# The value products of sparse attention, issued in eight rows of eight instead of sixteen rows of four

## The chip, the cores and the metric

One core of a Trainium2 chip (trn2) runs the whole layer. The metric is the device time of one execution in microseconds; the kernel before has a median of 1277.29 us over 3 runs (1276.85 to 1277.38).

## What the reference computes

One decoder layer (sequence 256, width 2048, all float32): a mixer, cross-attention to 256 memory tokens, and a gated MLP, each followed by a layer norm. The mixer projects the input and feeds three groups side by side: a diagonal state-space model (S5), stick-breaking attention, and NSA, attention with 16 query heads in 4 groups that share keys and values. NSA is the part that matters here. Its three branches (compressed keys, selected blocks, sliding window) are added with gates:

```python
p_s = masked_softmax(s_s, (dist_s >= 0)[:, :, None])
o_s = jnp.einsum('bgrqm,bgqmd->bqgrd', p_s.astype(vs.dtype), vs)
...
p_w = masked_softmax(s_w, mask_w)
o_w = jnp.einsum('bgrqk,bkgd->bqgrd', p_w.astype(vwb.dtype), vwb)
...
o = gb[..., 0:1] * o_c + gb[..., 1:2] * o_s + gb[..., 2:3] * o_w
```

With 256 tokens there are 4 blocks of 64, all of which are selected, and the window of 512 covers every earlier token, so the selected and the window branch are both plain causal attention, each with its own keys and values. The change is in their products of probabilities and values.

## The kernel before, in words

The program is written with a tile framework. Its planner puts the instructions of each engine in a fixed order when the kernel is built: it simulates the engines and issues, of what is ready, what has the best priority. Priorities go by lanes: `first`, then `split` (loads and the splitting of weights), `mixer` (attention and the like), and `proj` (the products of the projections), which so fills what the others leave free. `after(a, b)` adds that `a` is issued after `b`, without a semaphore; `in_row(row)` does it for a list, each after the one before. An engine runs its instructions in the order that was fixed.

The projections multiply float32 values split into a high and a low part: ScalarE casts a chunk of 1024 columns of weights to `hi` (line 304), VectorE takes the rest as `lo` (line 305), and three products are issued for each piece (`mm3`, lines 319 to 321, tokens moving; `mm3x`, lines 327 to 329, weights moving). Chunks come through four `raw` buffers and three each of `hi` and `lo`.

In the NSA stage 16 heads are worked through as 4 quads of 4. For each quad there are two branches `b` (0 is the selected one, which also gives the scores of the compressed keys, 1 the window), and in each branch two groups `gl` with two heads `r` each: 16 pairs of heads. For a head, TensorE forms scores (lines 1044 and 1045, into one of two `mx` banks), VectorE adds the bias and takes minima (1048, 1050), ScalarE the exponentials (1060, 1062), VectorE scales by gate and sum (1065 to 1069), TensorE transposes three blocks into one of two alternating banks `op` and `pb` (1074), and ScalarE copies them to a `pt` tile of 128 x 384 (1076). The products of line 1081 then multiply 64 columns of values `vv` (the weights) with `pt` (moving, 256 or 128 columns); head `r` = 0 writes partitions 0 to 63 of the bank `pa`, head 1 partitions 64 to 127, and group `gl` its own 256 columns. A float32 product is two load and two product records in the profile. At a quad's end the compressed branch is added (transposes 1092, copy 1096, products 1098), and `pa` is copied to `mix` (1101, 1102).

Projections fill the rest of this stage: the queries of NSA, `mix_out(0)` (first half of the output projection) and `memory_k` (keys of the memory, whose results `xk` are copied at line 1132). `mix_out(1)` comes behind the stage and reads NSA's `mix`. The stick-breaking stage before (`stick_breaking`) has four rows of its own at line 855, made with `in_row` and a dependency on ScalarE's last exponential.

Of the kernel before, what the change touches and what calls it, by code (L numbers as in the profile page):

```python
# [8 lines left out]
F32 = mybir.dt.float32  # L9
# [156 lines left out]
class Parts:  # L166
# [9 lines left out]
    def range(self, k, n):  # L176
        if k == 0 and self.first is not None:
            assert n == 1
            return self.first
        return self.tiles[k // self.n][:, k % self.n:k % self.n + n]  # L180
# [18 lines left out]
class Program:  # L199
# [322 lines left out]
    def mixer(self):  # L522
# [6 lines left out]
        with ExitStack() as nsa:  # L529
            self.nsq = pool(nsa, "nsq", 1)  # L530
            self.slabp = pool(nsa, "slabp", 1)
            with ExitStack() as s5:
                self.s5p = pool(s5, "s5p", 1, "right")
                self.s5w = pool(s5, "s5w", 2, "right")
                self.s5_tables()
                self.load_x()
                with ExitStack() as st:
                    self.sbp = pool(st, "sbp", 1)
                    self.sbw = pool(st, "sbw", 2)
                    self.stick_breaking()  # L540
                self.nsk = pool(nsa, "nsk", 1)
                self.nsa_compress()
                self.nsa_values()
                self.s5_out()
            self.resp = pool(self.ctx, "resp", 1, "right")
            self.R = self.resp.tile([128, 2, D], F32, name="R")
            self.mixq = pool(self.ctx, "mixq", 1, "right")
            self.mix += [self.mixq.tile([128, 4, 2, 256], F32R, name=f"mix{i}")
                         for i in range(2, 4)]
            with ExitStack() as st:  # L550
                self.nsp = pool(st, "nsp", 1, "right")
                self.nsw = pool(st, "nsw", 2, "right")
                self.nsa_queries()
                self.nsa()
# [452 lines left out]
    def nsa(self):  # L1007
        nc, a, V, S = self.nc, self.a, self.nc.vector, self.nc.scalar
        p, mm = self.nsp, nc.tensor.matmul
        vcb, vv, gate, ks, q = self.vcb, self.vv, self.gate, self.ks, self.nq  # L1010
        slab = self.slab
        self.after(S.activation(gate, gate, ACTF.Exp, scale=-1.0), self.table)
        V.tensor_scalar(gate, gate, 1.0, None, ALU.add)
        V.reciprocal(gate, gate)


        def qcol(h):
            return 4 * (h // 8) + 2 * (h // 4 % 2) + h % 2


        pc = p.tile([128, 2, NH, 32], F32, name="pc")
        nc.gpsimd.memset(pc, 0.0)
        tcs = [p.tile([128, 2, 4, NC_], F32, name=f"tcs{i}") for i in range(2)]
        for t in tcs:
            nc.gpsimd.memset(t[:, 0], BIG)
        halves = lambda t: t.rearrange("p (c k) -> p c k", c=2)
        for quad in range(4):
            o = self.pq.tile([128, 2, 256], F32, name="pa")
            start = [None, None]
            for b in range(2):  # L1030
                n = 128 if b else 128 + NK
                for gl in range(2):
                    h0, v = 4 * quad + 2 * gl, 4 * b + 2 * (quad // 2) + gl
                    sums = self.nsw.tile([128, 2, 2], F32, name="sums")
                    pes, pts = [], []
                    for r in range(2):
                        h = h0 + r
                        kh, kl = (k[:, h // 8, gl].rearrange("p c n -> p (c n)") for k in ks[b])
                        t = qcol(h)
                        z = self.mx.tile([128, 512], F32, name="mx")  # L1040

                        for qt, m in enumerate((256, n + 128)):
                            qs, zs = slice(128 * qt, 128 * qt + 128), z[:, qt * n:qt * n + m]
                            mm(zs, q[:, t, gl, qs], kh[:, 0:m], start=True, stop=False)  # L1044
                            mm(zs, q[:, t, gl, qs], kl[:, 0:m], start=False, stop=True)  # L1045
                        tt = self.nsw.tile([128, 384], F32, name="tt")
                        mn = self.nsw.tile([128, 2], F32, name="mn")
                        V.tensor_tensor_reduce(tt[:, 0:128], z[:, 0:128], slab[:, h, 128:256],
                                               1.0, 3e38, ALU.add, ALU.min, mn[:, 0:1])
                        V.tensor_tensor_reduce(halves(tt[:, 128:384]),  # L1050
                                               halves(z[:, n:3 * n])[:, :, 0:128],
                                               halves(slab[:, h, :]), 1.0, 3e38, ALU.add, ALU.min,
                                               mn[:, 1:2])
                        if b == 0:
                            for qt in range(2):
                                V.tensor_add(tcs[quad % 2][:, qt, 2 * gl + r, 0:NB[qt]],
                                             z[:, 128 + qt * n:128 + qt * n + NB[qt]],
                                             slab[:, h, 159 - 128 * qt:256:16])
                        pe = self.nsw.tile([128, 384], F32, name="pe", bufs=3)
                        S.activation(pe[:, 0:128], tt[:, 0:128], ACTF.Exp, scale=-1.0,  # L1060
                                     bias=mn[:, 0:1], accum_out=sums[:, r, 0:1])
                        S.activation(pe[:, 128:384], tt[:, 128:384], ACTF.Exp, scale=-1.0,
                                     bias=mn[:, 1:2], accum_out=sums[:, r, 1:2])
                        pes.append(pe)
                    V.reciprocal(sums, sums)
                    V.tensor_mul(sums, sums, gate[:, :, h0:h0 + 2, 1 + b].rearrange("p q r -> p r q"))
                    for r, pe in enumerate(pes):
                        V.tensor_scalar(pe[:, 0:128], pe[:, 0:128], sums[:, r, 0:1], None, ALU.mult)
                        V.tensor_scalar(pe[:, 128:384], pe[:, 128:384], sums[:, r, 1:2], None,
                                        ALU.mult)  # L1070
                        ps = self.turn()
                        for c in range(3):
                            cs = slice(c * 128, c * 128 + 128)
                            last = nc.tensor.transpose(ps[:, cs], pe[:, cs], self.ident)
                        pt = self.nsw.tile([128, 384], F32, name="pt", bufs=3)
                        S.copy(pt, ps[:, 0:384])
                        pts.append(pt)

                    for c, (k0, k1) in enumerate(((0, 256), (256, 384))):
                        for r, pt in enumerate(pts):  # L1080
                            ins = mm(o[64 * r:64 * r + 64, gl, 128 * c:256], vv[:, c, v, :],  # L1081
                                     pt[:, k0:k1], start=start[r] is None, stop=False,
                                     skip_group_check=True)
                            if c == 0:
                                self.after(ins, start[r] or last)
                                start[r] = start[r] or ins
                if b == 0:
                    self.softmax(tcs[quad % 2], gate[:, :, 4 * quad:4 * quad + 4, 0],
                                 pc[:, :, 4 * quad:4 * quad + 4, 0:NC_])
            ps = self.turn()  # L1090
            for qt in range(2):
                nc.tensor.transpose(ps[:, qt * 128:qt * 128 + 128],
                                    pc[:, qt, 4 * quad:4 * quad + 4, :].rearrange(
                                        "p r n -> p (r n)"), self.ident)
            pt = self.nsw.tile([128, 384], F32, name="pt", bufs=3)
            S.copy(pt[:, 0:256], ps[:, 0:256])
            for gl in range(2):
                mm(o[:, gl, :], vcb[:, quad // 2, 2 * gl:2 * gl + 2, :].rearrange("p r d -> p (r d)"),
                   pt[:, 0:256], start=False, stop=True, skip_group_check=True)
            m = self.mix[2 + quad // 2][:, quad % 2:4:2]  # L1100
            S.copy(m[:, :, 0, :], o)
            V.tensor_sub(m[:, :, 1, :], o, m[:, :, 0, :].bitcast(F32))
# [267 lines left out]
```

## Time and profile before

| what | us |
|---|---|
| median of 3 runs | 1277.29 |
| the profiled execution, its own time | 1276.8 |
| its span, first to last instruction | 1274.6 |
| mean granted TensorE clock over the span | 0.994 of full speed |
| NSA stage, from the span's start | 268 to 398 |

The times of the rows below are of the one profiled execution and count from its span's start. Its own time is 2.2 us longer than the span; the median of the runs is 0.5 us above it. PE is TensorE's matmul, PEld its weight loads, DVE is VectorE, ACT ScalarE, SP the queue that issues most loads. The ends of matmuls are modelled, so two that follow each other overlap in the rows in order of time; the chain of waits gives each only the time until the next.

### The profile page before, as it was taken

The page shows a single profiled execution, that of the slowest core. Times are in us where ns is not written, and L with a number is a line of the kernel's source. Part 1 is how long each engine was busy: PE and PEld are TensorE (multiplying, and loading weights), DVE is VectorE, ACT ScalarE, POOL GpSimd, SP SyncE. Part 2 cuts the span into 40 slices and gives each one's busy share as a digit, 9 for nine tenths or more (in the row PEclk, how much of TensorE's full clock was granted, in tenths as well). Part 3 has the DMA queues.
Part 4 walks back from the last instruction along what each step waited for, and adds up shares of the span by engine and source line. Part 5 has one row for each costly group of instructions (what it writes and reads, how often), then busy time and mean ns, then how long its engine had stood idle before and what let it go on. Part 6 is the DMA issues. An engine that isn't in the chain of part 4 may idle for free.

```text
span 1274.6 us, 23037 instructions
## 1 busy us (share of the span) xinstructions
PE 1242.8 (98%) x9222; PEld 1151.6 (90%) x9222; DVE 878.8 (69%) x1507; ACT 660.5 (52%) x1032; POOL 19.0 (1%) x34
## 2 busy tenths in 40 slices
PE   7999999999999999899999999999999999999996
PEld 7788889997788999799999999999999988888896
DVE  7799997876765766866666666666666654444557
ACT  6884446565663366365555555555555543334342
POOL 0200000100000000000000000000000000000000
PEclk9999999999999999999999999999999999999998
DMA  8654247664454655355666666666566766656573
GB/s 307 196 167 150 84 130 239 213 197 141 133 204 160 193 196 169 113 164 191 196 192 192 196 193 191 196 194 190 196 192 192 262 192 190 196 188 199 187 237 132
DMA packets 67350, 237.37 MB, mean 186 GB/s; under 512 B 7787, under 2 KB 8604, under 8 KB 66476
## 3 DMA queue, kind: packets, MB, share of 16 engines
q1 hardware_dynamic: 64720, 230.21, 55.9%
q0 software_dynamic: 1424, 4.33, 1.5%
q8 instruction: 72, 1.18, 0.4%
q10 hardware_dynamic: 1100, 1.38, 0.3%
q14 instruction: 34, 0.28, 0.1%
HBM read 231.82 MB, written 2.49 MB: 184 GB/s over the span
## 4 chain that ended last, share of the span: by engine, by line
PE 86%; DVE 6%; DMA 3%; ACT 3%; issue 2%; POOL 0%; DVEq 0%; ACTq 0%; POOLq 0%
PE pj L321 16%; PE pj L319 16%; PE pj L320 16%; PE pj L328 10%; PE pj L327 10%; PE pj L329 10%; PE pa L1081 2%; DVE s5m L191 1%; DVE lo L305 1%; DMA s5us<-Ec 1%; DVE s5z L191 1%; DMA raw<-in_win_u 1%; ACT hi L304 1%; PE mx L1044 1%; PE mx L1045 1%
## 5 line engine op out<-in xcount | busy, mean ns | idle before, releaser
L305 DVE TENSOR_TENSOR lo<-raw,hi 128x1024 fp32r<-128x1024 f32 (+2 forms) x403 | 488.1, 1211 | 330.4 <-ACT hi L304 329.2
L304 ACT CAST hi<-raw 128x1024 fp32r<-128x1024 f32 (+2 forms) x403 | 419.6, 1041 | 500.2 <-PE pj L320 268.1
L320 PE MATMUL pj<-mix,hi 128*128 128x256 f32 x1380 | 382.4, 277 | 0.0
L319 PE MATMUL pj<-mix,hi 128*128 128x256 f32 x1380 | 381.9, 277 | 0.0
L321 PE MATMUL pj<-mix,lo 128*128 128x256 f32 x1380 | 381.3, 277 | 0.0
L319 PEld LDWEIGHTS pj<-mix,hi 128*128 128x128 f32 x1380 | 259.5, 188 | 0.2
L320 PEld LDWEIGHTS pj<-mix,hi 128*128 128x128 f32 x1380 | 259.4, 188 | 0.1
L321 PEld LDWEIGHTS pj<-mix,lo 128*128 128x128 f32 x1380 | 259.4, 188 | 0.0
L319 PE MATMUL pj<-A,hi 128*128 128x256 f32 x496 | 139.6, 284 | 6.7 <-ACT hi L304 6.1
L321 PE MATMUL pj<-A,lo 128*128 128x256 f32 x496 | 137.6, 284 | 3.7 <-DVE lo L305 3.7
L320 PE MATMUL pj<-A,hi 128*128 128x256 f32 x496 | 138.6, 282 | 0.0
L319 PEld LDWEIGHTS pj<-A,hi 128*128 128x128 f32 x496 | 94.4, 191 | 9.4 <-ACT hi L304 6.6
L321 PEld LDWEIGHTS pj<-A,lo 128*128 128x128 f32 x496 | 92.9, 191 | 7.0 <-DVE lo L305 4.9
L328 PE MATMUL pj<-lo,A 128*128 128x512 f32 (+2 forms) x288 | 96.0, 334 | 1.0 <-DVE lo L305 1.0
L328 PE MATMUL pj<-lo,act 128*128 128x512 f32 (+1 forms) x280 | 96.3, 345 | 0.0
L329 PE MATMUL pj<-hi,act 128*128 128x512 f32 (+1 forms) x280 | 96.3, 345 | 0.0
L329 PE MATMUL pj<-hi,A 128*128 128x512 f32 (+2 forms) x288 | 95.8, 334 | 0.0
L320 PEld LDWEIGHTS pj<-A,hi 128*128 128x128 f32 x496 | 94.7, 192 | 0.8 <-issue 0.8
L327 PE MATMUL pj<-hi,A 128*128 128x512 f32 (+2 forms) x288 | 91.4, 334 | 0.6 <-ACT hi L304 0.6
L327 PE MATMUL pj<-hi,act 128*128 128x512 f32 (+1 forms) x280 | 89.3, 345 | 0.0
L328 PEld LDWEIGHTS pj<-lo,A 128*128 128x128 f32 x288 | 54.1, 188 | 7.8 <-DVE lo L305 1.5
L329 PEld LDWEIGHTS pj<-hi,A 128*128 128x128 f32 x288 | 54.2, 188 | 5.8 <-issue 0.8
(321 smaller groups left out, 1792.2 us busy)
## 6 DMA issues: line engine op xcount, KB each, us to landing
raw<-in_w_up SPq DMA_DIRECT2D x176, 512.0 KB, 4.4
raw<-in_w_down SPq DMA_DIRECT2D x92, 512.0 KB, 4.4
raw<-in_win_c SPq DMA_DIRECT2D x48, 512.0 KB, 4.1
raw<-in_w_out SPq DMA_DIRECT2D x32, 512.0 KB, 3.4
raw<-in_win_sv SPq DMA_DIRECT2D x8, 512.0 KB, 4.5
raw<-in_wk_m SPq DMA_DIRECT2D x8, 512.0 KB, 4.1
raw<-in_wv_m SPq DMA_DIRECT2D x8, 512.0 KB, 3.6
raw<-in_wq SPq DMA_DIRECT2D x8, 512.0 KB, 3.4
```

Source lines behind the costliest of these rows:

```text
L191: ins = getattr(self.engine, name)(*args, **kw)
L304: self.last_hi = nc.scalar.copy(hi[:, :n], raw[:, :n])
L305: self.last_lo = nc.vector.tensor_sub(lo[:, :n], raw[:, :n], hi[:, :n].bitcast(F32))
L319: mm(ps, hi, ah, start=start, stop=False)
L320: mm(ps, hi, al, start=False, stop=False)
L321: self.last_mm = mm(ps, lo, ah, start=False, stop=stop)
L327: mm(ps, ah, hi, start=start, stop=False)
L328: mm(ps, ah, lo, start=False, stop=False)
L329: self.last_mm = mm(ps, al, hi, start=False, stop=stop)
L1044: mm(zs, q[:, t, gl, qs], kh[:, 0:m], start=True, stop=False)
L1045: mm(zs, q[:, t, gl, qs], kl[:, 0:m], start=False, stop=True)
L1081: ins = mm(o[64 * r:64 * r + 64, gl, 128 * c:256], vv[:, c, v, :], pt[:, k0:k1], start=start[r] is None, stop=False, skip_group_check=True)
```

## The change

The products of a branch of a quad are issued after both of its groups have their four `pt` tiles, as one row of eight: for each of the two column pieces `c`, group 0 head 0, group 0 head 1, group 1 head 0, group 1 head 1. The row is put in order by `in_row`, and its first product waits, with a semaphore, for the last of the four copies (`copied`). Number, shapes and operands of the products stay as they were. The pool of `pt` tiles has five buffers in place of three.

```diff
@@ nsa() @@
             for b in range(2):
                 n = 128 if b else 128 + NK
+                pts = []
                 for gl in range(2):
-                    h0, v = 4 * quad + 2 * gl, 4 * b + 2 * (quad // 2) + gl
+                    h0 = 4 * quad + 2 * gl
                     sums = self.nsw.tile([128, 2, 2], F32, name="sums")
-                    pes, pts = [], []
+                    pes = []
...
-                        pt = self.nsw.tile([128, 384], F32, name="pt", bufs=3)
-                        S.copy(pt, ps[:, 0:384])
+                        pt = self.nsw.tile([128, 384], F32, name="pt", bufs=5)
+                        copied = S.copy(pt, ps[:, 0:384])
                         pts.append(pt)
 
-                    for c, (k0, k1) in enumerate(((0, 256), (256, 384))):
-                        for r, pt in enumerate(pts):
-                            ins = mm(o[64 * r:64 * r + 64, gl, 128 * c:256], vv[:, c, v, :],
+                row = []
+                for c, (k0, k1) in enumerate(((0, 256), (256, 384))):
+                    for gl in range(2):
+                        for r, pt in enumerate(pts[2 * gl:2 * gl + 2]):
+                            ins = mm(o[64 * r:64 * r + 64, gl, 128 * c:256],
+                                     vv[:, c, 4 * b + 2 * (quad // 2) + gl, :],
                                      pt[:, k0:k1], start=start[r] is None, stop=False,
                                      skip_group_check=True)
                             if c == 0:
                                 self.after(ins, start[r] or last)
                                 start[r] = start[r] or ins
+                            row.append(ins)
+                self.tc.add_manual_dep(row[0].ins, copied.ins.name, mybir.DependencyInfo(
+                    mybir.DependencyClass.Sync, mybir.DependencyReason.DATA), reason="in one row")
+                self.in_row(row)
...
-            pt = self.nsw.tile([128, 384], F32, name="pt", bufs=3)
+            pt = self.nsw.tile([128, 384], F32, name="pt", bufs=5)
             S.copy(pt[:, 0:256], ps[:, 0:256])
```

## Rows read from the trace of the kernel before

**Rows 1.** The page: the chain that ended last, shares of the span by line.
```profile
PE pj L321 16%; PE pj L319 16%; PE pj L320 16%; PE pj L328 10%; PE pj L327 10%; PE pj L329 10%; PE pa L1081 2%; DVE s5m L191 1%; DVE lo L305 1%; DMA s5us<-Ec 1%; DVE s5z L191 1%; DMA raw<-in_win_u 1%; ACT hi L304 1%; PE mx L1044 1%; PE mx L1045 1%
```
**Rows 2.** Windows: stretch, length, busy of PE, PEld, DVE, ACT, POOL, clock, DMA.
```profile
268.00:398.00 130.00, 129.05 (x870) 106.74 (x871) 94.28 (x343) 79.03 (x208) 0.00 (x0) 1.00 0.46 158
...
600.00:1200.00 600.00, 600.00 (x4499) 569.41 (x4498) 365.77 (x464) 292.85 (x380) 0.00 (x0) 1.00 0.62 197
```
**Rows 3.** Waits of SP's queue and DVE, 268 to 398: total, times, longest.
```profile
SPq L276 <- DVE lo L305: 71.2, 16, 7.6
...
DVE sums L1065 <- ACT pe L1062: 16.6, 9, 3.5
```
**Rows 4.** Groups by line, ACT, 268 to 398: busy, mean ns, idle before.
```profile
L304 ACT CAST hi<-raw 128x1024 fp32r<-128x1024 f32 x27 | 28.2, 1044 | 19.9 <-PE pj L329 14.1 <-PE pj L320 5.9
```
**Rows 5.** Line 1076, 268 to 398: what ended ACT's idle time, us, times.
```profile
  PE pb L1074: 11.4, 6
  PE op L1074: 8.8, 5
```
**Rows 6.** Groups by line, PE, 268 to 398.
```profile
L1081 PE MATMUL pa<-pt,vv 128*64 128x128 f32 (+1 forms) x128 | 22.2, 344 | 0.0
```
**Rows 7.** Chain of waits, 255 to 400, pieces of line 1081: start, us.
```profile
276.71 0.57 PE pa L1081 x2
278.52 0.79 PE pa L1081 x5
...
314.10 0.80 PE pa L1081 x8
```
**Rows 8.** PE in order of time, several stretches: start, us, instructions.
```profile
105.14 0.86 PE L855 MATMUL op<-sbe,sbv 128*64 128x256 f32 x6
...
106.37 0.43 PE L855 MATMUL op<-sbe,sbv 128*64 128x128 f32 x2
...
278.45 0.86 PE L1081 MATMUL pa<-pt,vv 128*64 128x256 f32 x6
...
288.82 0.38 PE L1074 MATMUL pb<-cst,pe 128*128 128x128 f32 x2
...
390.80 0.86 PE L1081 MATMUL pa<-pt,vv 128*64 128x256 f32 x6
391.60 0.39 PE L319 MATMUL pj<-A,hi 128*128 128x256 f32 x1
...
398.04 0.40 PE L327 MATMUL pj<-hi,mix 128*128 128x512 f32 x1
```
**Rows 9.** Chain of waits, projections before and behind line 1081.
```profile
276.59 0.11 PE pj L321
...
277.28 0.32 PE pj L319
...
279.31 0.31 PE pj L319
```
**Rows 10.** Chain of waits, a quad's products of line 1098.
```profile
336.78 0.86 PE pa L1098 x4
```
**Rows 11.** Line 1081, its weight loads: duration ns, least, median, greatest.
```profile
L1081 PEld LDWEIGHTS pa<-pt,vv x128: 132/136/137, 276.6 to 391.3; 128*64 128x64 f32 x128
```
**Rows 12.** PEld in order of time, from 313.95.
```profile
314.03 0.63 PEld L1081 LDWEIGHTS pa<-pt,vv 128*64 128x64 f32 x8 [0.37 <-DVE sums L1066]
```
**Rows 13.** Groups by line, PE, 100 to 200: the stick-breaking rows.
```profile
L855 PE MATMUL op<-sbe,sbv 128*64 128x256 f32 (+1 forms) x32 | 3.9, 340 | 0.5 <-ACT sbe L848 0.5
```
**Rows 14.** DVE in order of time, from 387; in brackets idle before.
```profile
390.91 1.09 DVE L1132 COPY xk<-pj 128x256 f32<-128x256 f32 x3 [2.05 <-PE pb L1092]
...
395.56 0.69 DVE L1102 TENSOR_TENSOR mix<-pa,mix 128x512 fp32r<-128x512 f32 x1 [2.43 <-ACT mix L1101]
```
**Rows 15.** ACT in order of time, two stretches.
```profile
290.11 0.47 ACT L1076 COPY pt<-pb 128x384 f32<-128x384 f32 x1
...
387.88 0.49 ACT L1076 COPY pt<-op 128x384 f32<-128x384 f32 x1
```

## The prediction

> **What bounds the kernel now.** I read the page first, then the stages, then the chain of waits inside the one stage that the diff touches. In the page's chain that ended last, TensorE's (PE's) lines 319 to 321 and 327 to 329, the projections, hold 3 x 16 + 3 x 10 = 78% of the span, and the touched products of line 1081 hold 2% [rows 1]. The windows view shows how even this is: in the NSA stage, 268 to 398 us, PE is busy 129.05 of 130 us at granted clock 1.00, while VectorE (DVE) has 94.28 and ScalarE (ACT) 79.03; from 600 to 1200 PE is busy 600 of 600 [rows 2]. In the NSA stage its own small work is spread over a stream of projection products, and these fill every hole. So here a microsecond that PE no longer needs is a microsecond off the end, if two things hold: the softmax chain on DVE and ACT keeps up with the quicker PE, and the loads do.
>
> The loads first. In this stage SP's queue waits 71.2 us for DVE's `lo` [rows 3], which frees a load buffer; DMA moves at 0.46 of its share [rows 2]. Loads wait for buffers, not PE for loads. ACT's cast of the next weights waits 19.9 us for PE to give a buffer back [rows 4]: the preparation of weights, too, stands on PE.
>
> The chain second. ACT waits 8.8 + 11.4 = 20.2 us, at 5 + 6 = 11 of the 32 copies to `pt`, for transposes that PE has not yet issued [rows 5]; DVE waits 16.6 us for exponentials that stand behind those copies [rows 3]. The chain is waiting for PE's order, not the other way round. PE itself shows 0.0 idle before line 1081 [rows 6].
>
> **What one group of products costs now.** A product is two records on PE, one for each weight load. The chain of waits shows a group of four products (eight records, two heads into the two halves of the array's columns) in two forms. In 13 of 16 groups the first head's first product goes off alone as "x2", other work follows, then the other three go ("x5" in the chain, six records in the order of time); in 3, the first groups of the second, third and fourth quad, the eight stand together; one of each kind is shown [rows 7, 8]. Each visit costs its own time and a slow return to the projections: the matmul behind takes 0.32 or 0.31 us in the chain where its like take 0.11 [rows 9].
> - alone: 0.57 + (0.32 - 0.11) = 0.78 us
> - the six: 0.79 + (0.31 - 0.11) = 0.99 us
> - the eight together, with the same return: 0.80 + 0.21 = 1.01 us
>
> The eight cost no more than the six because the halves run beside each other: the lone first product hides beside the other head's. Columns agree: four full-width records of 256 columns take 0.86 us [rows 10], 0.215 each. One half has two such records and two of half the width: 2 x 0.215 + 2 x 0.108 = 0.645 us, and 1.01 - 0.645 = 0.36 us is the price of going in and out. Alone: 0.43 + 0.35.
> Before, in all: 13 x (0.78 + 0.99) + 3 x 1.01 = 26.0 us.
>
> **The change, part by part.**
> *One row of eight.* Alternating heads keep both halves filled, so a row has two groups' columns and one way in and out: 1.01 + 0.645 = 1.65 us; eight rows make 13.2 us. PE saves 26.0 - 13.2 = 12.8 us: about 10 from 13 lone visits, 2.9 from eight other visits fewer. Number and shapes of products, loads and copies are unchanged.
>
> *A rule of the skill, weighed.* Eight weight loads of about 0.136 us each, 1.09 in sum [rows 11], end within 0.63 us of the first one's start [rows 12], and their products take 0.80 us [rows 7]: loads run beside loads and products. The Trainium skill ("TensorE: Matmul & The Clock Gate", Part 3, The mechanism) says that a weight load overlaps running matmuls only when its row group differs; all these products use all 128 rows, so by it the loads would add to the time. The trace disagrees, and the sum goes by the trace; by the rule the change would lose, as worked out under the rivals.
>
> *The wait at the row's head.* Its first product now waits for the last of four copies. Behind it in PE's queue stand projections, the next heads' scores and transposes; for these wait DVE's minima, ACT's copies, the casts. Below: 0, since PE idles 0.0 before line 1081 [rows 6]. Above: the stick-breaking stage has four rows made in this form (in order, waiting for ACT's last result), and there PE idled 0.5 us before them in total [rows 13]. All of that at one row and the same at each of eight gives 4.0 us; its mean, 0.125 us a row, gives 1.0. I take 1.0, the same form being the nearest row.
>
> *Products of the first pair move later,* by one pair, some 8 us. Only line 1098 and the copy to `mix` need them, at the quad's end, and these wait for the second pair anyhow: no cost. The last quad's mix is written at 395.56 to 396.25, the next consumer, `mix_out(1)`, starts at 398.04 [rows 8, 14], and its first chunks read other tiles.
>
> *Two more buffers.* Four copies are held until the row; the fifth takes the next head's copy or line 1096's. They run nothing. Were they missing, ACT would stand at the next copy: the 0.48 us of a copy and what waits for it.
>
> Sum: 1276.8 (the profiled execution, span 1274.6 and 2.2 around it) - 12.8 + 1.0 = 1265.0. The median of the runs stands 0.5 higher: **1265.5 us**. Bounds of the wait, and up to 1 us for the return cost of rows that end at transposes, make 1263.5 to 1268.5.
>
> **The rivals.**
> A. *The chain shows.* 11 of 32 copies waited for PE with 20.2 us in all, more than 12.8 [rows 5]; but if they stand for 11 of the 16 pairs, 5 pairs have no such cover. If these give their share back, 5/16 x 12.8 = 4.0 us: 1269.5. For: in `xk` too, DVE copies three finished blocks only at 390.91, released by the last quad's transposes, and the fourth block starts at 391.60 [rows 8, 14], so the stage's end has little play. Against: DVE would be busy 94.28 of some 117 us, 80%.
>
> B. *Halves not beside each other* in the longer row. 16 records in sequence: 8 x 0.215 + 8 x 0.108 + 0.36 = 2.94 us, 23.5 in all, 2.5 saved: 1274.8. Against: the eight at 0.80 [rows 7].
>
> C. *Loads show.* 16 loads x 0.136 = 2.2 us more a row, 17.4 in all, against 12.8: 4.6 lost, 1281.9. Against: the 0.63 us [rows 12]. This is what the skill's rule quoted above would make of it.
>
> D. *The row stands too early in PE's queue: slower.* Place: each row's head. After transposes that end at 289.20, the second copy ends at 290.58, as exponentials stand before it [rows 8, 15]: 1.4 us, and 2.4 with a 1.04 us cast [rows 4] in front. If rows are queued right behind the transposes, with nothing between, eight times this is 11.2 to 19.2 us: 1264.5 + 11.2 = 1275.7 to 1283.7. It decides from 12.8/8 = 1.6 us a row (gain gone). Against: the last group's copies end at 388.37 and its six records go at 390.80 [rows 8, 15]; projections stand between, and none of 16 groups kept PE idle [rows 6].
>
> E. *The rows do not come out whole.* One of the stick-breaking rows goes as six records and, after another line's, two [rows 8]. Eight extra visits of 0.36 leave 9.9 us of gain: 1268.4.
>
> **How the numbers follow.** Forecast 0.64, A 0.13, E 0.05, B 0.05, C 0.03, D 0.10. The forecast's own range is 1263.5 to 1268.5; with A and E up to 1271 it holds 0.82, and I open the low end to 1262.8, for PE work saved that the sum of visits misses. 0.2%, 2.6 us, is about what a measurement of this kernel can tell from no change. Faster: forecast, A, E and 0.02 of B, 0.84. Same: 0.03 of B and 0.06 of D, 0.09. Slower: C and 0.04 of D, 0.07.
>
> **What would show it.** Line 1081 as eight pieces of "x16" (or near) and about 1.44 us in the chain, the matmul behind at 0.3; no "x2" pieces; PE idle before line 1081 about 1 us; the start of `mix_out(1)` near 386 in place of 398.04; ACT's 20.2 us for transposes down to about half. Pieces of 2.7 us mean B or C; idle before line 1081 of over 4 us means D; idle before lines 1044, 1074 or 319 in the stage means A. The forecast is wrong above all if the queue's order in the stage changes so that projections run out before the last quad ends.

## The result, and the profile after

The kernel with the change takes 1265.42 us (median of 6 runs, 1264.3 to 1266.71), the kernel before beside it 1276.91 us (6 runs, 1275.76 to 1277.38). The ratio is 0.9911, 95% interval 0.9900 to 0.9922: 1276.91 x 0.0089 = 11.4 us, or 0.9%, faster. Forecast was 1265.5 us, 11.8 us below the 1277.29 us of before that were known then.

The profiled execution has a span of 1262.4 us. The windows view of it, with the columns of [rows 2]:

```profile
268.00:386.00 118.00, 116.57 (x870) 104.22 (x869) 92.77 (x331) 77.55 (x203) 0.00 (x0) 1.00 0.51 171
...
600.00:1190.00 590.00, 590.00 (x4403) 559.11 (x4402) 359.35 (x457) 287.04 (x371) 0.00 (x0) 1.00 0.60 197
```

The reader is to see that the stage which ran from 268 to 398 us ends at 386: 870 product records in 118 us, where before the same number, equal also shape by shape, took 130 [rows 2]. PE's busy time for them fell from 129.05 to 116.57 us, by 12.5 us, and its idle time rose from 0.95 to 1.43 us. Behind the stage PE is as full as before, so nothing of this is given back.

The products of line 1081 are line 1084 now. The chain of waits, 255 to 400 (start, us, what), against [rows 7]:

```profile
284.92 1.45 PE pa L1084 x16
286.37 0.48 PE op L1075 x3
286.85 0.33 PE pb L1075 x3
...
334.03 0.86 PE pa L1106 x4
334.89 0.33 PE pb L1075 x3
...
344.92 1.45 PE pa L1084 x16
346.38 0.32 PE pj L329
346.69 0.12 PE pj L327
...
378.18 1.52 PE pa L1084 x16
```

Eight pieces of sixteen records, seven of 1.45 us and the last of 1.52; predicted were 1.44. No pieces of two are left. The return is there too: the projection behind a row takes 0.32 us where the next takes 0.12, three transposes behind a row 0.48 where the next three take 0.33. PE in order of time around the first row and at the stage's end, against [rows 8]:

```profile
284.52 0.40 PE L327 MATMUL pj<-hi,mix 128*128 128x512 f32 x1
284.85 1.52 PE L1084 MATMUL pa<-pt,vv 128*64 128x256 f32 x16
286.31 0.55 PE L1075 MATMUL op<-cst,pe 128*128 128x128 f32 x3
...
376.49 0.61 PE L1075 MATMUL pb<-cst,pe 128*128 128x128 f32 x3 [1.25 <-DVE pe L1069]
376.95 0.61 PE L1075 MATMUL op<-cst,pe 128*128 128x128 f32 x3
377.72 0.44 PE L1100 MATMUL pb<-cst,pc 128*128 128x128 f32 x2 [0.17 <-ACT pt L1077]
378.18 1.52 PE L1084 MATMUL pa<-pt,vv 128*64 128x256 f32 x16
...
386.06 0.40 PE L327 MATMUL pj<-hi,mix 128*128 128x512 f32 x1
```

`mix_out(1)` starts at 386.06 in place of 398.04: 11.98 us of the difference between the spans (12.2) are there by then. The brackets show the only idle time of PE in the stage, 1.25 + 0.17 us. It stands not at a row's head but before the last transposes, at the stage's very end, where no projection is left to fill. Before, PE idled once in the stage too, at its start, and that wait is gone:

```profile
268.95 0.39 PE L1044 MATMUL mx<-kh,nq 128*128 128x256 f32 x1 [0.97 <-DVE tcs L1056]
```

ACT's waits in the stage (total, times, longest), against [rows 5]:

```profile
ACT pt L1077 <- PE pb L1075: 10.5, 6, 3.6
...
ACT pt L1077 <- PE op L1075: 4.2, 4, 1.5
```

ACT still waits for PE's transposes, 14.7 us in place of 20.2: the softmax chain has used 5.5 us of its play (time it spends waiting, and can lose without holding PE up). Over most of the stage it has not become the limit. At the end it has: the chain of waits leaves PE for 2.2 us, from 374.25 to 376.49:

```profile
374.25 0.35 ACT pt L1077
...
374.63 0.49 ACT pe L1061 x2
375.12 0.50 ACT pe L1063 x2
...
376.05 0.30 DVE pe L1069
```

### The profile page after: what moved, and what is told of

It reads as the page before. It is cut to its first block, busy times and chain, and to the rows that moved or that the text cites. A ratio compares the mean times of both kernels' runs of the same rounds, so it can differ in the third digit from the quotient of the medians.

```text
span 1262.4 us, 23018 instructions
## 1 busy us (share of the span) xinstructions
PE 1229.5 (97%) x9222; PEld 1149.0 (91%) x9222; DVE 878.8 (70%) x1507; ACT 660.2 (52%) x1032; POOL 19.0 (2%) x34
## 4 chain that ended last, share of the span: by engine, by line
PE 86%; DVE 7%; DMA 3%; ACT 2%; issue 1%; POOL 0%; SPq 0%; DVEq 0%; ACTq 0%
PE pj L319 17%; PE pj L321 17%; PE pj L320 17%; PE pj L328 10%; PE pj L327 10%; PE pj L329 10%; DVE s5m L191 1%; DVE lo L305 1%; DMA s5us<-Ec 1%; PE pa L1084 1%; DVE s5z L191 1%; DMA raw<-in_win_u 1%; ACT hi L304 1%; PE mx L1045 1%; PE mx L1046 1%
```

## The experiments

The theory is the prediction's: PE's work in this stage counts one to one, and what is saved are lone products beside which half of the array's columns stands empty, and visits to this kind of product (a visit is one stretch in which PE leaves its other work for them). Its rivals are the number of rows alone, the later place of the products, the buffers, and a chain that becomes the limit. Ten kernels were run; each ratio is to the kernel before, run beside it on the same chip, so it need not be the quotient of two medians of this text. The chain of waits counts only records that take time of their own: five products, ten records, show there as "x8".

| kernel | us, median | ratio | 95% interval |
|---|---|---|---|
| the change | 1265.42 | 0.9911 | 0.9900 to 0.9922 |
| whole rows of four, five buffers | 1267.99 | 0.9936 | 0.9923 to 0.9948 |
| whole rows of four, three buffers | 1267.98 | 0.9928 | 0.9916 to 0.9941 |
| before, five buffers | 1278.45 | 1.0020 | 1.0011 to 1.0029 |
| rows of eight, not bound | 1276.16 | 0.9998 | 0.9989 to 1.0007 |
| rows of eight, heads apart | 1273.58 | 0.9974 | 0.9965 to 0.9983 |
| the change, four buffers | 1266.2 | 0.9914 | 0.9901 to 0.9928 |
| the change, products twice | 1275.2 | 0.9984 | 0.9976 to 0.9993 |
| the change, six transposes in a row | 1268.64 | 0.9934 | 0.9921 to 0.9947 |
| the change, pc elsewhere | 1265.4 | 0.9914 | 0.9900 to 0.9927 |
| the change, six transposes and pc elsewhere | 1266.01 | 0.9915 | 0.9902 to 0.9929 |

**Whole rows of four.** The kernel before, with each group's four products bound in the way of the change, and five buffers.

```diff
-                        pt = self.nsw.tile([128, 384], F32, name="pt", bufs=3)
-                        S.copy(pt, ps[:, 0:384])
+                        pt = self.nsw.tile([128, 384], F32, name="pt", bufs=5)
+                        copied = S.copy(pt, ps[:, 0:384])
...
+                    row = []
...
+                            row.append(ins)
+                    self.tc.add_manual_dep(row[0].ins, copied.ins.name, mybir.DependencyInfo(
+                        mybir.DependencyClass.Sync, mybir.DependencyReason.DATA), reason="in one row")
+                    self.in_row(row)
...
-            pt = self.nsw.tile([128, 384], F32, name="pt", bufs=3)
+            pt = self.nsw.tile([128, 384], F32, name="pt", bufs=5)
```

> Sixteen rows of four, each whole and bound as the change binds its rows of eight, with five buffers: only the length of the row differs from the change. Theory (visits): a whole row of four costs 1.01 us, so 16.2 us in place of the 26.0 of before, 9.8 us of PE work saved; with some 1 us of waits a gain of 8.8 us, ratio to before 0.9931. Lines after a row that are transposes may make a visit cheaper, so up to 9.8 us. Rival (the gain comes from halving the number of rows): only the visits saved by joining two rows count, 8 x 0.36 = 2.9 us of the change's 11.4, so rows of four would give the rest only if the lone products cost what the chain shows; if they do not, rows of four gain nothing, ratio 1.00.

Ratio 0.9936, forecast 0.9931. In the chain of waits all sixteen rows are whole:

```profile
277.70 0.80 PE pa L1082 x8
286.36 0.80 PE pa L1082 x8
```

So whole rows carry 1276.77 x 0.0064 = 8.2 us, and the step from four to eight the rest: 0.9936 - 0.9911 is 3.2 us by the middles, where 2.9 was forecast. The two intervals stand a hair apart (0.9922 and 0.9923), so the second share is measured less surely than the first.

**Before, with five buffers.**

```diff
-                        pt = self.nsw.tile([128, 384], F32, name="pt", bufs=3)
+                        pt = self.nsw.tile([128, 384], F32, name="pt", bufs=5)
...
-            pt = self.nsw.tile([128, 384], F32, name="pt", bufs=3)
+            pt = self.nsw.tile([128, 384], F32, name="pt", bufs=5)
```

> The kernel before with five buffers for the copies in place of three, nothing else. Theory: the buffers run nothing and no copy waited for one, so the time is that of before within 0.1%. Rival (buffers carry part of the gain, because copies no longer wait for products): ACT's idle time before the copies, 20.2 us in the trace of before, falls, and 1 to 4 us of the 11.4 come from here, ratio 0.997 to 0.999.

Neither: 1.0020, a loss of some 2.6 us. Buffers carry none of the gain. They let the planner place some products and transposes otherwise; in the profiled execution `mix_out(1)` starts at 398.56 in place of 398.04, and the span is 0.9 us longer, so it shows a third of the loss. Even that is not shown to come from the stage: by 262 us, before the stage, PE had done 1874 records there against 1881, some 0.8 us less. Where the loss lies was not found. Whole rows of four were therefore run with three buffers too:

> The whole rows of four with three buffers in place of five. Rows of four with five buffers stand at ratio 0.9936, and before with five buffers at 1.002. Theory (more buffers only change the order in which the planner places the stage, with chance effects of some 2 us either way): 0.9936 within 0.002, without a set sign. Rival (two more buffers cost 0.2% by themselves): 0.9916.

0.9928 beside 0.9936: no difference that these intervals can tell. Against this run the step from four to eight is worth 2.2 us by the middles, and its interval, from 0.9916, reaches into the change's. A fixed cost of the buffers is not shown, and the loss in the kernel before stays unexplained.

**Rows of eight, not bound.** The change's loops and buffers without the two statements that bind the row.

```diff
-                self.tc.add_manual_dep(row[0].ins, copied.ins.name, mybir.DependencyInfo(
-                    mybir.DependencyClass.Sync, mybir.DependencyReason.DATA), reason="in one row")
-                self.in_row(row)
```

> The change's loops and five buffers, but without the dependency on the last copy and without the fixed order: each product goes when its own copy is there. In the order as built, a branch's eight products now go as 2, 1 and 5 or as 1, 1, 1 and 5. By the visits: a pair beside each other 0.43 + 0.36 = 0.79 us, a lone one 0.78, the five 2 x 0.215 + 4 x 0.108 + 0.36 = 1.22; that is 2.79 or 3.56 us a branch, 25.4 us in all against 26.0 before. Theory (whole rows carry the gain): 0.6 us gained, ratio 0.9995. Rival (the later place of the products and the joining of both groups carry it): most of the change's 11.4 us stays, ratio 0.992.

0.9998, as forecast: the gain is gone. The chain of waits shows the pieces that were named, here of a branch with 2, 1 and 5 products:

```profile
280.77 0.58 PE pa L1084 x4
...
284.68 0.58 PE pa L1084 x2
...
286.74 1.01 PE pa L1084 x8
```

The first line is a reading lesson: two products beside each other take the same 0.58 us as the single one below them. The later place and the common loop buy nothing that can be told from zero; the row must be whole.

**Heads apart.** The order within a row is turned, so that neighbours use the same half of the columns.

```diff
-                for c, (k0, k1) in enumerate(((0, 256), (256, 384))):
-                    for gl in range(2):
-                        for r, pt in enumerate(pts[2 * gl:2 * gl + 2]):
+                for r in range(2):
+                    for c, (k0, k1) in enumerate(((0, 256), (256, 384))):
+                        for gl in range(2):
+                            pt = pts[2 * gl + r]
```

> The change's eight rows of eight, but within a row the four products of the first head come first and then the four of the second, so that neighbours use the same half of the array's columns. Theory (the halves run beside each other only where neighbours alternate): a row takes one half after the other but for one overlap, 2 x 1.29 - 0.215 + 0.155 = 2.5 us in the chain in place of 1.45, eight rows lose 8.5 us, and the gain on before falls to some 3 us, ratio 0.9977. Rival (PE finds the other half's products by itself, however they are ordered): rows stay at 1.45 us, ratio 0.991.

0.9974 against a forecast of 0.9977. Two rows in the chain of waits, and the first of them in order of time, with all its sixteen records:

```profile
287.21 2.36 PE pa L1085 x14
303.49 2.36 PE pa L1085 x14
```

```profile
287.14 2.44 PE L1085 MATMUL pa<-pt,vv 128*64 128x256 f32 x16
```

2.36 us for the same products that take 1.45 us when heads alternate. PE did not reach past its neighbours in the queue for work for the empty half; neighbours must bring it.

**Four buffers.**

```diff
-                        pt = self.nsw.tile([128, 384], F32, name="pt", bufs=5)
+                        pt = self.nsw.tile([128, 384], F32, name="pt", bufs=4)
...
-            pt = self.nsw.tile([128, 384], F32, name="pt", bufs=5)
+            pt = self.nsw.tile([128, 384], F32, name="pt", bufs=4)
```

> The change with four buffers for the copies in place of five: the row holds all four, so the next copy has to wait until the row has gone. Theory (PE's order sets the time and the copies have play): the row goes some 2 to 5 us after its last copy and the next pair's transposes later still, so no copy waits long; ratio to before as the change's 0.991, within 0.0015. Rival (the buffers are needed): ACT stands at the first copy behind each row and passes it on to PE, up to 1 us a row, 8 us in all, ratio 0.997.

0.9914, as the change. ACT's copies at the quads' ends do wait for the row now:

```profile
ACT pt L1104 <- PE pa L1084: 4.1, 4, 1.4
```

These 4.1 us cost no time that can be seen. The fifth buffer isn't needed; four hold the row.

**Products twice.** Each product of a row is issued a second time behind the eight, so the output counts the two branches double; only the time is of use.

```diff
+                again = row
+                row = list(again)
+                for c, (k0, k1) in enumerate(((0, 256), (256, 384))):
+                    for gl in range(2):
+                        for r, pt in enumerate(pts[2 * gl:2 * gl + 2]):
+                            row.append(mm(o[64 * r:64 * r + 64, gl, 128 * c:256],
+                                          vv[:, c, 4 * b + 2 * (quad // 2) + gl, :],
+                                          pt[:, k0:k1], start=False, stop=False,
+                                          skip_group_check=True))
```

> The change with each product of the row issued a second time behind the first eight, so the two plain branches count double in the output. Only PE's columns grow, without a further visit: 2 x 0.645 = 1.29 us a row, 10.3 us in all. Theory (a microsecond of PE in this stage is one at the end): 10.3 us slower than the change, ratio to before 0.9911 + 0.0081 = 0.999, rows of 1.45 + 1.29 = 2.74 us in the chain. Rival (in the change the chain on DVE and ACT is already the limit in part, so that more PE work hides): clearly less than 10.3 us, say half, ratio 0.995.

0.9984: 0.0073 above the change, 9.3 us of the 10.3. The chain of waits has the second half of a row as its own piece:

```profile
285.37 1.45 PE pa L1084 x16
286.82 1.30 PE pa L1097 x16
```

1.30 us without a further way in, so the 0.15 us within the 1.45 are paid once a row, and 8 x 1.30 = 10.4 us of PE work come out as 9.3 us of time. The two intervals together leave nearly 2 us either way. In the profiled execution `mix_out(1)` starts at 395.87, 9.8 us after the change's 386.06, and PE's idle time in the stage is 0.8 us in place of 1.4: some of the added work filled a gap. PE's time is the stage's time, within what this can tell.

**Six transposes in a row.** If visits cost whatever their kind, the transposes of a pair should gain by the same binding.

```diff
+                    six, banks = [], [self.turn(), self.turn()]
+                    for ps, pe in zip(banks, pes):
                         for c in range(3):
...
+                            six.append(last)
+                    self.tc.add_manual_dep(six[0].ins, scaled.ins.name, mybir.DependencyInfo(
+                        mybir.DependencyClass.Sync, mybir.DependencyReason.DATA), reason="six in a row")
+                    self.in_row(six)
+                    for ps in banks:
+                        pt = self.nsw.tile([128, 384], F32, name="pt", bufs=5)
+                        copied = S.copy(pt, ps[:, 0:384])
+                        pts.append(pt)
```

> The change, and the six transposes of a pair bound into one row in the same way: both heads are scaled first, the first transpose waits for the last scale. In the order as built the 96 transposes go in 18 visits in place of 34. In the trace of the change a visit of three takes some 0.66 us from the matmul before it to the second one behind it, where two projections take 0.23 and three transposes of 128 columns 0.17: 0.26 us for the visit. Theory (each visit to another kind of work costs, whatever the kind): 16 visits fewer, 2 to 4 us below the change, ratio to before 0.988 to 0.9895. Rival (only column halves make the difference, and the copies that now start later cost the chain as much): as the change or above, ratio 0.991 or more.

The theory failed: 0.9934, some 3 us above the change. The waits of PE in the stage:

```profile
PE pb L1076 <- DVE pe L1070: 2.7, 1, 2.7
PE pa L1090 <- ACT pt L1083: 0.7, 1, 0.7
PE pb L1106 <- ACT pt L1083: 0.3, 1, 0.3
```

3.7 us idle in place of the change's 1.4, at its end again, where both heads' scaling must be done before the first transpose and no projection stands by. That is 2.3 of the 3 us.

The saving is missing as well, and the expectation's price is why: it took three transposes for 0.17 us. The change's own chain of waits has 0.33 (the second fence of the section on the result), and it shows transposes between projections:

```profile
367.38 0.12 PE pj L319
367.49 0.11 PE pb L1075
367.60 0.12 PE pj L320
367.73 0.12 PE pj L321
367.85 0.22 PE pb L1075 x2
368.06 0.11 PE op L1075
368.17 0.13 PE pj L319
```

One transpose takes 0.11 us, two 0.22, three 0.33, and the projection behind them 0.12 or 0.13, about what it takes among its like. A visit of transposes has no way in or out worth saving. Nor do the four full-width float32 products of line 1106 have a slow return: three transposes behind them take 0.33. The price of a visit belongs to the products on half of the columns.

**pc elsewhere.** Projections run out there because `xk`, the memory keys, lie where the stage's tiles were and wait for its last transposes of `pc` ([rows 14] show that wait). Moving two small tiles lets `xk` go earlier; it was run for the change and for the six transposes.

```diff
-        pc = p.tile([128, 2, NH, 32], F32, name="pc")
+        pc = self.nsw.tile([128, 2, NH, 32], F32, name="pc", bufs=1)
         nc.gpsimd.memset(pc, 0.0)
-        tcs = [p.tile([128, 2, 4, NC_], F32, name=f"tcs{i}") for i in range(2)]
+        tcs = [self.nsw.tile([128, 2, 4, NC_], F32, name=f"tcs{i}", bufs=1) for i in range(2)]
```

> The change, with the tiles of the compressed scores (pc and tcs) moved to the pool of small NSA tiles, so that the memory keys xk, which later take the place of the query tiles, no longer wait for the last quad's transposes of pc. In the order as built the last quad's work now stands between projections to its end. Theory (in the change PE idles 1.2 + 0.2 us at the stage's end because projections have run out): these 1.4 us go, ratio to before 0.990. Rival (the last quad's chain is the limit itself, and mix_out(1) now waits for its mix): as the change, 0.991.

> The same move, with the six transposes of a pair in one row. With the transposes bound alone PE idled 3.7 us at the stage's end and the ratio to before was 0.9934. Theory (fewer visits of transposes do save, and the loss came where projections had run out): the idle time goes and 1 to 3 us below the change remain, ratio 0.9885 to 0.990. Rival (rows of transposes save nothing, since a transposing row costs PE the same columns and their copies start later): as the change at best, 0.991 or more.

The windows view of the change, of pc elsewhere, and of both, one fence each:

```profile
262.00:400.00 138.00, 136.57 (x984) 121.81 (x984) 104.94 (x356) 87.02 (x217) 0.00 (x0) 1.00 0.53 178
```

```profile
262.00:400.00 138.00, 138.00 (x995) 123.67 (x994) 106.02 (x357) 87.27 (x218) 0.00 (x0) 1.00 0.54 181
```

```profile
262.00:400.00 138.00, 138.00 (x995) 123.76 (x994) 104.70 (x355) 87.34 (x218) 0.00 (x0) 1.00 0.52 178
```

PE has no idle time left in this stretch and gets 11 more records done, all of them short projections, about 11 x 0.113 = 1.2 us. In the time this isn't seen: 0.9914 has 0.990 and 0.991 in its interval, so it doesn't decide between the two expectations. The profiled execution can't decide either: by 262 us it had done 1871 records against the change's 1882, so it was as much behind before the stage as it gained in it. With the six transposes the move brings 0.9934 to 0.9915; the intervals overlap, but the direction and the idle time that is gone agree with the cause named. The last two fences show the same 995 records; by shape, the last has three long projections fewer (0.23 us each) and three short ones more (0.11 us each). Binding the transposes saved no PE time that can be seen. No version that was run beats the change.

## Why the prediction was right

- *The bound.* A microsecond of PE in the stage was taken as one at the end. Shown: 9.3 of 10.4 us added came out, with nearly 2 us either way, and the change's own 12 us were whole at `mix_out(1)`.
- *Cost of a group by visits.* Alone 0.78, six 0.99, eight 1.01 us. Whole rows of four were forecast from these at 0.9931 and measured 0.9936; pieces as they come, 0.9995 and 0.9998. The sum's larger term, about 10 us from 13 lone visits, is borne out at 8.2 us measured, 9.2 with three buffers (8.8 forecast with waits).
- *A row of eight.* 1.65 us with its return, 1.44 in the chain; measured 1.45. The return of 0.21 was taken for every visit; it is 0.20 behind the row that a projection follows, and 0.15 where transposes follow. Rival B fell here and, from the other side, with heads apart: without alternation the row does take 2.36 us. Rival C fell with the same number: sixteen loads of some 0.136 us, 2.2 in sum, fit into 1.45.
- *The wait at the row's head.* The term was 1.0 us, from the stick-breaking rows. Measured: 0 before line 1084, and 1.4 us before the last transposes and their `pc` sisters; as the 0.97 us at the stage's start are gone, idle time grew by 0.5 us in all. That the size is near is luck: the place was not the one named. The wait belongs to rival A's mechanism, the thin end of the stage, at a third of its price, and it is what the prediction's last sentence warned of: projections ran out before the last quad ended. Rival D did not happen: PE never stood at a row's head.
- *Buffers.* Costed at nothing beside holding the row. Four do the same as five. That five alone cost the kernel before 0.2% was not foreseen.
- *Later products of the first pair.* Costed at nothing; `mix_out(1)` started 12 us sooner, so nothing waited for them.
- *Play of the chain.* ACT's waiting for transposes was to fall to about half, and fell only from 20.2 to 14.7 us, so the chain kept more play than forecast, except at the stage's end.

Terms together: 12.8 - 1.0 = 11.8 us forecast. In the profiled executions PE's busy time fell by 12.5 us and its idle time grew by 0.5, which makes 12.0; by the runs' ratio it is 11.4. Both terms were a little too large, and their errors partly cancel.

## What to carry to other kernels

Where a small kind of product is mixed into a full stream, price it by the visit: the pieces of the chain of waits plus the slow matmul behind, if it is slow. Read this for each kind: here products on half of the columns paid for a visit, and transposes and full-width products did not. Products that use half of the array's columns are worth their time only beside neighbours that use the other half, and a planner that issues each as its operand is ready pulls them apart. Bind the row to its last operand. Before you bind more in that way, look for what fills the stage's end.

## What the runs showed of the hardware

Products in the two halves of the columns overlap only when they alternate in the queue: 1.45 us against 2.36 us for the same eight products. Sixteen weight loads of some 0.136 us each fit into such a row. The way in and out of it is about 0.36 us when projections stand on either side; once in, eight more products cost 1.30 us, as much as the columns of one half (2 x 0.645 us). Transposes of 128 columns paid no such price, 0.11 us each whether alone or three together, and joining 34 visits of them into 18 saved nothing visible.
